# One inference step of a hybrid encoder: scale products moved within a step, element-wise work moved between engines, a new order at the start

## The chip, the cores and the metric

One core of a Trainium2 chip runs the kernel. The metric is the device time of one execution in microseconds (us), the median of several runs. Engines are named as in the profile: PE is TensorE, with PEld its weight loads, DVE is VectorE, ACT is ScalarE, POOL is GpSimd, SP is the queue that issues the DMAs.

## The reference

One layer (DEPTH = 1) is computed for two groups of tokens that share the weights: a prompt of 256 and a sample of 32 tokens, both of width 2048. In short:

```python
def trunk_layer(x, mk, mv, past_k, past_v, lru_buf, lru_h, ssd_buf, ssd_h, ffn_buf, lp):
    m, st = hybrid_mixer(rmsnorm(x, lp['norm_mix']), past_k, past_v, lru_buf, lru_h, ssd_buf, ssd_h, lp)
    h = x + m
    h = h + cross_attn(rmsnorm(h, lp['norm_xattn']), mk, mv, lp['w_xq'], lp['w_xo'])
    f, ffn_new = conv_ffn(rmsnorm(h, lp['norm_ffn']), ffn_buf, lp['w_up'], lp['ffn_conv_w'], lp['ffn_conv_b'], lp['w_down'])
    return h + f, st + (ffn_new,)

def hybrid_mixer(xn, ...):
    proj = xn @ lp['w_in']          # 2048 -> 13840: q k v, lru x/gate, ssd z/xBC/dt, 3 merge gates
    o_a = stick_breaking(q, k_all, v_all, P)                       # 8 heads x 128
    o_b = rg_lru(causal_dwconv(lx, ...)) * gelu(lg)                # width 1024, conv of 4
    o_c = rmsnorm((ssd_chunked(silu(causal_dwconv(xbc, ...))) + d * xh) * silu(z))
    merged = sum over n of sigmoid(gate_n) * (branch_n @ w_branch[n])
    return merged @ lp['w_out'], states

def conv_ffn(xn, buf, w_up, cw, cb, w_down):
    u, buf_new = causal_dwconv(xn @ w_up, buf, cw, cb)             # 2048 -> 2 x 5632, conv of 3
    g, v = jnp.split(u, 2, axis=-1)
    return (jax.nn.silu(g) * v) @ w_down, buf_new
```

`rmsnorm` scales by the root of the mean square and a gain. `causal_dwconv` is a depthwise convolution over time that also returns the last inputs as a state. The prompt's memory (256 tokens) is normed and projected to keys and values; the sample has cached ones. All is float32. The outputs are the two normed results, the keys and values, and the states.

## The kernel before

Activations lie transposed: 128 features in the partitions, 256 + 32 = 288 tokens in a row, so a width of 2048 is 16 tiles. The weights stream from memory once, 1 MB at a time. A unit of this stream is an *item*. `items` is a written list, and `run_items` (L458) walks it.

An item of the f16 form (mode "h") is 128 x 2048 float32 weights. To keep float32 accuracy from f16 products, weights and activations are each split into a high part and a low part, and three products are added: high by high, high by low, low by high. The weights are first scaled by a power of two. Its exponent is worked out in a chain over four engines: ACT squares the whole item into `junk` with a sum per partition (`square_w`, L315); PE multiplies the sums with a matrix of ones, a product with one column, into `z` (`scale_mm`, L328; for a group of four items DVE adds the sums into `sum` first); DVE masks the exponent into `e` (`scale_e`, L338); ACT and POOL make `scale` and `inv` of it (`scale_w`, L342). Then follow the high part `wh` (`split_high`, L351: on DVE for every third item, else on ACT) and the low part `wl` on DVE (`split_low`, L366). `z` has one PSUM buffer. An item is 48 products with 288 columns.

An item of the f32r form (mode "r") is 128 x 1024 weights or less. Its parts are f32r numbers, with no square, no scale and no `z`. It is used while the norm is not known yet: the products take x times its gain, and the norm's factor `S` is applied when the result is read (`ev`, L523). The first `R_IN` = 6 projections of `w_in` and the first `R_UP` = 6 of `w_up` are of this form. Each is 48 products, in two or three items.

A *step* is the time of one item on PE. `stream` (L387) gives four parts p0 to p3, which `run_items` calls after each quarter of the item's products (an f32r item of 24 products has two stretches with two parts each). After each stretch `tick` (L425) lets every side step go one `yield` further; evictions, convolutions, attention heads, the scan and the splits of activations are such steps. p0 issues the high part of the second item ahead, p1 its low part, the load of the sixth item ahead and the product into `z` for the third ahead, p2 the square of the fourth ahead and `e`, p3 `scale` and `inv`. An item in `needs` that isn't over makes `finish` (L431) tick until it is.

The order on PE, ACT, DVE and POOL is the order in which the program writes the instructions, so an instruction that waits holds all that stand behind it on its engine. All DMAs, results and caches included, are issued on SP's queue. There are 5 weight buffers of 1 MB, 6 buffers for split parts, 55 activation tiles, 4 PSUM banks for projections and 3 for side work.

`conv` (L710) reads a projection in PSUM: DVE multiplies the taps by the two scales into `wt` and writes the state (`last`), ACT makes the first tap `cx`, DVE adds the others, and the bank is freed. `split_normed` (L1196) makes of a normed activation tile `t` (DVE), the f16 high part `h` (ACT) and the low part `l` (DVE, L283); it serves the inputs of `w_in`, `w_xq` and the f16 part of `w_up`. `normed_later` (L1158) adds squares of the residual for the next norm and, ahead of the FFN, makes its f32r parts `xh` (ACT) and `xl` (DVE).

The start is written out (L1654 to L1695): loads, splits of the first weights and of the inputs, squares of the 16 input tiles on ACT, 15 adds one after the other on POOL (L560), then the norm's products, for which PE waits in place.

Of the kernel before, what the change touches and what calls it, by code (L numbers as in the profile page):

```python
# [16 lines left out]
P = 128  # L17
# [3 lines left out]
D = 2048  # L21
# [32 lines left out]
R_IN, R_UP = 6, 6  # L54
# [42 lines left out]
class Group:  # L97


    def __init__(self, n):  # L100
        self.n, self.got, self.sq, self.scale, self.inv = n, 0, None, None, None

# [18 lines left out]
def encoder_step(ctx: ExitStack, tc: tile.TileContext, A):  # L121
# [228 lines left out]

    def split_high():  # L351
        it = items[split_at[0]]
        n = it.n
        split_at[0] += 1
        if it.mode == "r":
            it.h = wh_p.tile([P, 1024], F32R, tag="wh", name=nm("wh"))
            act(it.h[:, 0:n], it.raw[:, 0:n], AF.Copy)
        elif it.mode == "h":
            it.h = wh_p.tile([P, 2048], F16, tag="wh", name=nm("wh"))
            if split_at[0] % 3 == 0:  # L360
                V.tensor_scalar(it.h[:, 0:n], it.raw[:, 0:n], it.scale, None, ALU.mult)  # L361
            else:
                act(it.h[:, 0:n], it.raw[:, 0:n], AF.Copy, scale=it.scale)
        return it
# [22 lines left out]
    def stream(i):  # L387

        high, scales = [], []

        def p0():
            while split_at[0] < ahead(i, 2):
                high.append(split_high())

        def p1():
            for it in high:
                split_low(it)
            while raw_at[0] < ahead(i, NRAW + 1):
                fetch_w()
            while sc_at[0] < ahead(i, 3):  # L400
                it = scale_mm()
                scales.append(it)

        def p2():
            while sq_at[0] < ahead(i, 4):
                square_w()
            for it in scales:
                scale_e(it)

        def p3():  # L410
            for it in scales:
                scale_w(it)
        return p0, p1, p2, p3

    side = []
# [15 lines left out]
    def finish(get):  # L431
        while get() is None or not get().over:
            tick()
# [65 lines left out]
    def add_r(srcs, xh, xl, done, n=T, needs=(), pre=None):  # L499
# [3 lines left out]
        for c, x in enumerate(srcs):  # L503
            nk = x.shape[1] // P
            items.append(Item("r", [x], [still(u, xh, xl, n, k0, nk, 0, c == 0, c == len(srcs) - 1)],
                              needs=needs if c == 0 else (), pre=pre if c == 0 else None))
# [111 lines left out]
    def sb_evac(kind, h):  # L618
        def done(u):
            x = tt(name=kind)  # L620
# [5 lines left out]
            if kind == "v":  # L626
                sb["g", h] = spawn(sb_head(h))
        return done
# [81 lines left out]
    def conv(u, n, w, b, hist, last):  # L710
# [7 lines left out]
        else:  # L718
            wt = small("wt", 4)
            V.tensor_scalar(wt[:, 0:n], w, u.inv, u.inv2, ALU.mult, ALU.mult)  # L720
            w = wt
        tail = src[:, 257 - n:321 - n].rearrange("p (a b) -> p a b", b=32)[:, :, 0:n - 1]
        if u.inv is None:
            G.tensor_copy(last, tail)
        else:
            V.tensor_scalar(last, tail, u.inv, u.inv2, ALU.mult, ALU.mult)  # L726
# [431 lines left out]
    def normed_later(j, h, key, name, op, parts=None):  # L1158

        if parts:  # L1160
            act(parts[0][:, C], h, AF.Copy, scale=pc(name, j))
# [8 lines left out]
        if parts:  # L1170
            stt(parts[1][:, C], h, pc(name, j), f32(parts[0])[:, C], ALU.mult, ALU.subtract)
# [24 lines left out]
    def split_normed(op, xs, name, scale, n=T):  # L1196
# [4 lines left out]
        for i, x in enumerate(xs):  # L1201
            y = tt()
            stt(y[:, 0:n], x, g[:, i:i + 1], scale[:, 0:n], ALU.mult, ALU.mult)
            op.h[i], op.l[i] = split16(y[:, 0:n], n)
# [203 lines left out]
    def xo_evac(j, half):  # L1408
        def done(u):
# [5 lines left out]
            hh_[j], hl_[j] = tt(F32R, "xh"), tt(F32R, "xl")  # L1415
            yield
            yield from normed_later(j, h[:, C], "f", "g_ffn", op_f, (hh_[j], hl_[j]))
# [197 lines left out]
    def up(b):  # L1615
        j0, n = blocks[b]
        for j in range(j0, j0 + n):
            for i, done in ((j, up_g(j)), (NFF + j, up_v(j))):
                if 2 * j < R_UP:
                    add_r(two("w_up", i), hh_, hl_, done)  # L1620
# [52 lines left out]
    make_sb_masks()  # L1673
    for k in range(KD):
        if k >= 8:
            split_x([k])
        add_square(acc, xin[k][:, C], k == 0)
        if k == 9:
            run_items(0, 2)
        if k == 13:  # L1680
            run_items(2, 4)
    run_items(4, 6)
    spawn(gains("g_mix", gmix))
    run_now(norm_scale(acc, S, D))
# [158 lines left out]
```

## Time and profile before

| what | value |
|---|---|
| median of 3 runs | 2322.0 us (2319.89 to 2324.35) |
| profiled execution | 2324.89 us |
| its span | 2323.2 us |
| mean granted clock of PE | 0.97 |
| busy: PE, DVE, ACT, POOL | 2192.3, 1639.1, 1571.4, 312.8 us |
| bytes moved | 409.32 MB, mean 176 GB/s |

The span runs from the first to the last instruction of one profiled execution. A busy time is the sum over an engine's instructions; products on PE overlap, and their ends are modelled. The granted clock is a share of TensorE's full level. A wait in a row is idle time of an engine just before an instruction, put down to the instruction that ended last.

### The profile page before, as it was taken

What the parts mean: (1) busy time and instruction counts of PE and PEld (TensorE: products, weight loads), DVE (VectorE), ACT (ScalarE), POOL (GpSimd) and SP (SyncE); (2) the same over time, 40 slices, a digit from 0 to 9 for tenths busy, and PEclk for the clock granted to TensorE, in tenths of its full rate; (3) what the DMA queues carried; (4) which work ended last, traced back from release to release, by engine and by line L of the source; (5) the groups of instructions that cost most, each with busy time, mean ns of one, the idle gap of its engine ahead of it and who ended that gap; (6) DMA issues with size and microseconds to landing.
All of it is one profiled execution on the core that took longest, in us unless ns stands there. A gap on an engine that the chain in (4) does not pass through costs nothing.

```text
span 2323.2 us, 43464 instructions
## 1 busy us (share of the span) xinstructions
PE 2192.3 (94%) x17375; PEld 1739.6 (75%) x17375; DVE 1639.1 (71%) x2561; ACT 1571.4 (68%) x2261; POOL 312.8 (13%) x723
## 2 busy tenths in 40 slices
PE   6899978999899999899899999969999999999997
PEld 6788756777677777676587768867777777777776
DVE  5666776668875556765656556778887878878775
ACT  5666688777777685775555556657776767767674
POOL 3000001212232241132100000300000000000002
PEclk8899989999999999999899999979999999999999
DMA  7455434766556565565455554345555555555551
GB/s 234 160 177 165 159 121 145 241 222 215 167 190 202 186 214 189 160 216 169 160 182 183 183 177 166 110 145 182 164 185 179 182 182 174 175 180 180 182 183 62
DMA packets 134124, 409.32 MB, mean 176 GB/s; under 512 B 15264, under 2 KB 36896, under 8 KB 133920
## 3 DMA queue, kind: packets, MB, share of 16 engines
q1 hardware_dynamic: 133920, 406.53, 53.8%
q8 instruction: 136, 2.23, 0.4%
q14 instruction: 68, 0.56, 0.1%
HBM read 396.26 MB, written 10.21 MB: 175 GB/s over the span
## 4 chain that ended last, share of the span: by engine, by line
PE 74%; DVE 12%; ACT 9%; issue 3%; DMA 2%; POOL 1%; SPq 0%; POOLq 0%; DVEq 0%; ACTq 0%
PE mm L191 70%; DVE wl L194 4%; PE sd L191 3%; ACT wh L169 3%; ACT junk L169 2%; DVE cx L194 2%; ACT t L169 1%; ACT h L169 1%; ACT L169 1%; DVE wh L361 1%; DVE t L194 1%; POOL acc L560 1%; DMA wr<-in_w_xv 1%; DVE wl L370 0%; DVE l L283 0%
## 5 line engine op out<-in xcount | busy, mean ns | idle before, releaser
L191 PE MATMUL mm<-h,wh 128*128 128x288 f16 (+1 forms) x5072 | 1458.4, 288 | 4.9 <-ACT h L169 4.9
L191 PE MATMUL mm<-l,wh 128*128 128x288 f16 (+1 forms) x5072 | 1458.3, 288 | 1.2 <-DVE l L283 0.4
L191 PE MATMUL mm<-h,wl 128*128 128x288 f16 (+1 forms) x5072 | 1458.4, 288 | 0.0
L191 PEld LDWEIGHTS <-wh 128*128 128x128 f16 x10144 | 977.7, 99 | 275.2 <-issue 29.2
L194 DVE SCALAR_TENSOR_TENSOR wl<-wr,scale,wh 128x2048 f16<-128x2048 f32 x333 | 787.3, 2364 | 254.0 <-ACT wh L169 235.5
L169 ACT ACTIVATE junk<-wr 128x2048 bf16<-128x2048 f32 x333 | 632.4, 1899 | 2.5
L191 PEld LDWEIGHTS <-wl 128*128 128x128 f16 x5072 | 499.5, 98 | 130.2 <-issue 3.5
L169 ACT ACTIVATE wh<-wr,scale 128x2048 f16<-128x2048 f32 x222 | 443.2, 1996 | 83.4 <-PE mm L191 78.3
L275 POOL TENSOR_SCALAR inv<-e 128x1 int32<-128x1 int32 x337 | 84.0, 249 | 1678.2 <-DVE e L248 1605.7
L169 ACT ACTIVATE scale<-e 128x1 int32<-128x1 int32 x337 | 65.7, 197 | 218.7 <-DVE e L248 217.0
L194 DVE SCALAR_TENSOR_TENSOR cx<-mm,wt,cx 128x1 f32<-128x1 f32 (+4 forms) x346 | 141.9, 410 | 50.1 <-ACT cx L169 41.4
L361 DVE TENSOR_SCALAR wh<-wr,scale 128x2048 f16<-128x2048 f32 x111 | 144.1, 1298 | 32.5 <-ACT scale L169 30.4
L191 PE MATMUL z<-sq,bones 128*128 128x1 bf16 x317 | 53.1, 167 | 77.9 <-ACT junk L169 54.1
L194 DVE SCALAR_TENSOR_TENSOR xre<-mm,uinv,xre 128x288 f32<-128x288 f32 x144 | 72.8, 512 | 62.8 <-PE mm L191 43.9
L169 ACT ACTIVATE cx<-mm,par,wt 128x288 f32<-128x288 f32 x102 | 60.3, 591 | 57.7 <-DVE fcv L726 45.2
L560 POOL TENSOR_TENSOR acc<-acc,t 128x288 f32<-128x288 f32 x57 | 75.4, 1323 | 72.6 <-ACT t L169 70.8
L191 PE MATMUL mm<-xh,wh 128*128 128x288 f32 x192 | 65.7, 342 | 13.7 <-ACT wh L169 8.7
L191 PEld LDWEIGHTS <-bones 128*128 128x128 bf16 x337 | 32.8, 98 | 55.3 <-DVE e L248 46.3
L191 PE MATMUL mm<-xh,wl 128*128 128x288 f32 x192 | 63.9, 333 | 4.3 <-DVE wl L370 4.3
L191 PEld LDWEIGHTS mm<-xh,wh 128*128 128x128 f32 x192 | 42.4, 221 | 32.9 <-issue 17.9
L169 ACT ACTIVATE h<-t 128x288 f16<-128x288 f32 x48 | 21.1, 439 | 65.9 <-DVE t L194 65.9
L169 ACT ACTIVATE gate<-mm,uinv 128x288 f32<-128x288 f32 x48 | 23.7, 494 | 61.3 <-PE mm L191 58.7
(324 smaller groups left out, 1854.8 us busy)
## 6 DMA issues: line engine op xcount, KB each, us to landing
wr<-in_w_in SPq DMA_DIRECT2D x215, 512.0 KB, 4.4
wr<-in_w_up SPq DMA_DIRECT2D x176, 512.0 KB, 4.3
wr<-in_w_dn SPq DMA_DIRECT2D x80, 512.0 KB, 4.4
wr<-in_w_xv SPq DMA_DIRECT2D x64, 512.0 KB, 5.1
wr<-in_w_br SPq DMA_DIRECT2D x48, 512.0 KB, 4.5
wr<-in_w_xk SPq DMA_DIRECT2D x32, 512.0 KB, 4.5
wr<-in_w_out SPq DMA_DIRECT2D x32, 512.0 KB, 4.4
wr<-in_w_xq SPq DMA_DIRECT2D x32, 512.0 KB, 4.2
```

Source lines behind the costliest of these rows:

```text
L169: return nc.scalar.activation(out, in_, f, **kw)
L191: PE.matmul(out, lhsT, rhs, start=start, stop=stop, skip_group_check=True)
L194: V.scalar_tensor_tensor(out, a, s, b, op0, op1)
L275: G.tensor_scalar(s, e, float(UNSCALE_BITS + (more << 23)), None, ALU.add)
L361: V.tensor_scalar(it.h[:, 0:n], it.raw[:, 0:n], it.scale, None, ALU.mult)
L560: G.tensor_tensor(accum[:, 0:n], accum[:, 0:n], q[:, 0:n], ALU.add)
```

## The change

Seven edits, in the order of the diff: the first nine projections of `w_in` are f32r instead of six; half of the high parts go to DVE, except in the FFN and in 28 items from the SSD's first on, where it stays a third; the parts of a step are in another order, with `e`, `scale` and `inv` first (of the products of the step before), then the high parts, then low parts, loads and squares, and the products into `z` last; the taps are scaled by two POOL instructions a tick earlier, and the state is written by ACT; ahead of the FFN, POOL multiplies by the gain (`hg`), ACT rounds it to the high part, DVE subtracts, and the f32r items wait (`Ready`) until 8 and 16 tiles are written; the low parts `l` of `split_normed` go to POOL (those of the memory, L1244, stay on DVE); at the start the squares follow the splits, their adds alternate between POOL and DVE in two sums, and the norm is a side step, for which `sb_evac` waits. In `add_r` the preload of an item is moved to its last part.

```diff
--- before.py
+++ after.py
@@ -51,7 +51,7 @@
 RG_ENDS = (3, 7)
 NRAW, NWH, NT, NU, NS, NSD = 5, 6, 55, 66, 13, 3
 
-R_IN, R_UP = 6, 6
+R_IN, R_UP = 9, 6
 
 
 SLOT = 12
@@ -99,6 +99,20 @@
 
     def __init__(self, n):
         self.n, self.got, self.sq, self.scale, self.inv = n, 0, None, None, None
+
+
+class Ready:
+
+
+    def __init__(self, h, l, n):
+        self.h, self.l, self.n = h, l, n
+
+    def __call__(self):
+        return self
+
+    @property
+    def over(self):
+        return None not in self.h[:self.n] and None not in self.l[:self.n]
 
 
 class Step:
@@ -348,6 +362,10 @@
         elif it.mode == "h":
             it.scale, it.inv = g.scale, g.inv
 
+    def high_on_dve(i):
+
+        return i % 3 == 0 if i > i_ffn or i_ssd < i < i_ssd + 28 else i % 2 == 0
+
     def split_high():
         it = items[split_at[0]]
         n = it.n
@@ -357,7 +375,7 @@
             act(it.h[:, 0:n], it.raw[:, 0:n], AF.Copy)
         elif it.mode == "h":
             it.h = wh_p.tile([P, 2048], F16, tag="wh", name=nm("wh"))
-            if split_at[0] % 3 == 0:
+            if high_on_dve(split_at[0]):
                 V.tensor_scalar(it.h[:, 0:n], it.raw[:, 0:n], it.scale, None, ALU.mult)
             else:
                 act(it.h[:, 0:n], it.raw[:, 0:n], AF.Copy, scale=it.scale)
@@ -386,32 +404,33 @@
 
     def stream(i):
 
-        high, scales = [], []
+        high = []
 
         def p0():
+            for it in scales:
+                scale_e(it)
+            for it in scales:
+                scale_w(it)
+            scales.clear()
+
+        def p1():
             while split_at[0] < ahead(i, 2):
                 high.append(split_high())
 
-        def p1():
+        def p2():
             for it in high:
                 split_low(it)
             while raw_at[0] < ahead(i, NRAW + 1):
                 fetch_w()
-            while sc_at[0] < ahead(i, 3):
-                it = scale_mm()
-                scales.append(it)
-
-        def p2():
             while sq_at[0] < ahead(i, 4):
                 square_w()
-            for it in scales:
-                scale_e(it)
 
         def p3():
-            for it in scales:
-                scale_w(it)
+            while sc_at[0] < ahead(i, 3):
+                scales.append(scale_mm())
         return p0, p1, p2, p3
 
+    scales = []
     side = []
 
     def spawn(gen, first=False):
@@ -429,7 +448,7 @@
                 side.remove(s)
 
     def finish(get):
-        while get() is None or not get().over:
+        while not (get() and get().over):
             tick()
 
     def run_now(gen):
@@ -503,7 +522,7 @@
         for c, x in enumerate(srcs):
             nk = x.shape[1] // P
             items.append(Item("r", [x], [still(u, xh, xl, n, k0, nk, 0, c == 0, c == len(srcs) - 1)],
-                              needs=needs if c == 0 else (), pre=pre if c == 0 else None))
+                              needs=needs[c:c + 1], pre=pre if c == len(srcs) - 1 else None))
             k0 += nk
 
     def add_unit(srcs, op, done, n=T, needs=(), pre=None, more=0, both=False):
@@ -617,6 +636,8 @@
 
     def sb_evac(kind, h):
         def done(u):
+            while "S" not in sb:
+                yield
             x = tt(name=kind)
             ev(u, x[:, 0:T])
             free_mm(u)
@@ -625,6 +646,7 @@
                 load(A["kt" if kind == "k" else "vt"][h], x[:, 0:T])
             if kind == "v":
                 sb["g", h] = spawn(sb_head(h))
+            yield
         return done
 
     def sb_cache(h):
@@ -716,14 +738,16 @@
             ev(u, src[:, C])
             free_mm(u)
         else:
-            wt = small("wt", 4)
-            V.tensor_scalar(wt[:, 0:n], w, u.inv, u.inv2, ALU.mult, ALU.mult)
+            wt, both = small("wt", 4), small("both")
+            G.tensor_tensor(both, u.inv, u.inv2, ALU.mult)
+            G.tensor_tensor(wt[:, 0:n], w, both.to_broadcast([P, n]), ALU.mult)
             w = wt
+            yield
         tail = src[:, 257 - n:321 - n].rearrange("p (a b) -> p a b", b=32)[:, :, 0:n - 1]
         if u.inv is None:
             G.tensor_copy(last, tail)
         else:
-            V.tensor_scalar(last, tail, u.inv, u.inv2, ALU.mult, ALU.mult)
+            act(last, tail, AF.Copy, scale=both)
         act(x[:, C], src[:, C], AF.Identity, scale=w[:, n - 1:n], bias=b)
         yield
         for d in range(1, n):
@@ -1155,10 +1179,11 @@
             load(xre[j][:, C], A["xt"][j])
         return pre
 
-    def normed_later(j, h, key, name, op, parts=None):
+    def normed_later(j, h, key, name, op, parts=False):
 
         if parts:
-            act(parts[0][:, C], h, AF.Copy, scale=pc(name, j))
+            hg = tt()
+            G.tensor_scalar(hg[:, C], h, pc(name, j), 1.0, ALU.mult, ALU.mult)
         last = tt() if j == KD - 1 else None
         if j == 0:
             norm["acc"] = tt(name="acc")
@@ -1168,7 +1193,11 @@
             add_square(norm["acc"], h, j == 0)
         yield
         if parts:
-            stt(parts[1][:, C], h, pc(name, j), f32(parts[0])[:, C], ALU.mult, ALU.subtract)
+            hi, lo = tt(F32R, "xh"), tt(F32R, "xl")
+            act(hi[:, C], hg[:, C], AF.Copy)
+            yield
+            V.tensor_sub(lo[:, C], hg[:, C], f32(hi)[:, C])
+            hh_[j], hl_[j] = hi, lo
         if last:
             yield
             yield from norm_scale(norm.pop("acc"), S, D, more=[last])
@@ -1201,7 +1230,10 @@
         for i, x in enumerate(xs):
             y = tt()
             stt(y[:, 0:n], x, g[:, i:i + 1], scale[:, 0:n], ALU.mult, ALU.mult)
-            op.h[i], op.l[i] = split16(y[:, 0:n], n)
+            h, l = ut("h"), ut("l")
+            act(h[:, 0:n], y[:, 0:n], AF.Copy)
+            G.tensor_tensor(l[:, 0:n], y[:, 0:n], h[:, 0:n], ALU.subtract)
+            op.h[i], op.l[i] = h, l
             yield
 
     gain = {}
@@ -1412,9 +1444,8 @@
             free_mm(u)
             if half == 0:
                 return
-            hh_[j], hl_[j] = tt(F32R, "xh"), tt(F32R, "xl")
-            yield
-            yield from normed_later(j, h[:, C], "f", "g_ffn", op_f, (hh_[j], hl_[j]))
+            yield
+            yield from normed_later(j, h[:, C], "f", "g_ffn", op_f, True)
         return done
 
 
@@ -1617,7 +1648,7 @@
         for j in range(j0, j0 + n):
             for i, done in ((j, up_g(j)), (NFF + j, up_v(j))):
                 if 2 * j < R_UP:
-                    add_r(two("w_up", i), hh_, hl_, done)
+                    add_r(two("w_up", i), hh_, hl_, done, needs=[Ready(hh_, hl_, 8 * c + 8) for c in range(2)])
                 else:
                     add_unit(two("w_up", i), op_f, done, needs=[lambda: xa.get("f")] if 2 * j == R_UP and i == j else ())
 
@@ -1671,17 +1702,27 @@
     split_x(range(6, 8))
     split_w()
     make_sb_masks()
+    run_items(0, 2)
+    split_x(range(8, 12))
+    run_items(2, 4)
+    split_x(range(12, 16))
+
+    acc2 = tt(name="acc")
     for k in range(KD):
-        if k >= 8:
-            split_x([k])
-        add_square(acc, xin[k][:, C], k == 0)
-        if k == 9:
-            run_items(0, 2)
-        if k == 13:
-            run_items(2, 4)
+        q = (acc, acc2)[k] if k < 2 else tt()
+        act(q[:, C], xin[k][:, C], AF.Square)
+        if k > 1:
+            a = (acc, acc2)[k % 2]
+            (G, V)[k % 2].tensor_tensor(a[:, C], a[:, C], q[:, C], ALU.add)
     run_items(4, 6)
     spawn(gains("g_mix", gmix))
-    run_now(norm_scale(acc, S, D))
+
+    def first_norm(a, b):
+        yield 2
+        yield from norm_scale(a, S, D, more=[b])
+        sb["S"] = True
+    spawn(first_norm(acc, acc2), True)
+    acc2 = None
     run_items(6, 8)
     xs = [t[:, C] for t in xin]
     xa["x"] = spawn(split_normed(op_x, xs, "g_mix", S))
```

## Rows read from the trace of the kernel before

**Rows 1.** Page, part 1: busy us, share, instructions of the engines.

```profile
PE 2192.3 (94%) x17375; PEld 1739.6 (75%) x17375; DVE 1639.1 (71%) x2561; ACT 1571.4 (68%) x2261; POOL 312.8 (13%) x723
```

**Rows 2.** Waits of PE, whole span: total us, times, longest.

```profile
PE z L191 <- ACT junk L169: 54.1, 16, 8.4
PE z L191 <- DVE e L248: 22.9, 16, 3.8
PE z L191 <- DVE sum L242: 8.3, 4, 4.4
PE mm L191 <- ACT wh L169: 8.7, 4, 4.7
...
PE sd L191 <- POOL acc L560: 2.2, 2, 1.7
```

**Rows 3.** Windows by stage: length, busy by engine, PEclk, DMA share, GB/s.

```profile
0.00:115.00 115.00, 87.11 (x553) 77.03 (x554) 71.78 (x112) 66.23 (x111) 20.48 (x38) 0.85 0.62 197
...
280.00:410.00 130.00, 109.80 (x808) 82.67 (x807) 89.26 (x163) 109.90 (x162) 16.07 (x39) 0.92 0.42 137
...
1080.00:1160.00 80.00, 68.01 (x423) 42.76 (x421) 52.14 (x72) 46.50 (x64) 7.85 (x22) 0.89 0.49 158
...
1480.00:1560.00 80.00, 61.38 (x407) 55.92 (x405) 55.36 (x96) 42.83 (x70) 9.51 (x17) 0.85 0.41 130
1560.00:2280.00 720.00, 718.54 (x5951) 573.19 (x5950) 584.07 (x999) 517.52 (x706) 40.22 (x169) 1.00 0.54 177
2280.00:2323.00 43.00, 29.65 (x238) 23.04 (x235) 24.50 (x44) 20.32 (x41) 14.01 (x20) 0.90 0.16 56
```

**Rows 4.** Chain of waits, 40 us and more in: start, us, what.

```profile
29.32 9.63 PE mm L191 x72
...
2210.99 5.90 PE mm L191 x48
```

**Rows 5.** Timeline of PE at 309 us: start, length, [idle before <-releaser].

```profile
309.24 0.16 PE L191 MATMUL z<-sq,bones 128*128 128x1 bf16 x1 [5.34 <-ACT junk L169]
```

**Rows 6.** Instructions by shape, whole span: count, busy, mean ns, idle before.

```profile
L194 DVE SCALAR_TENSOR_TENSOR wl<-wr,scale,wh 128x2048 f16<-128x2048 f32 x333 | 787.3, 2364 | 254.0 <-ACT wh L169 235.5 <-DMA wr<-in_w_up 4.8 <-DMA wr<-in_w_xv 4.1
...
L169 ACT ACTIVATE wh<-wr,scale 128x2048 f16<-128x2048 f32 x222 | 443.2, 1996 | 83.4 <-PE mm L191 78.3 <-issue 3.3
L361 DVE TENSOR_SCALAR wh<-wr,scale 128x2048 f16<-128x2048 f32 x111 | 144.1, 1298 | 32.5 <-ACT scale L169 30.4 <-DMA wr<-in_w_xo 1.6 <-PE z L191 0.3
...
L370 DVE TENSOR_TENSOR wl<-wr,wh 128x1024 fp32r<-128x1024 f32 x21 | 26.6, 1270 | 9.0 <-ACT wh L169 8.0 <-DMA wr<-in_w_in 0.5 <-PE mm L191 0.5
...
L720 DVE TENSOR_SCALAR wt<-par,inv,inv 128x3 f32<-128x3 f32 x82 | 23.0, 280 | 0.0
```

**Rows 7.** The start: timeline of POOL, a window, PE's wait up to 115 us.

```profile
12.27 16.24 POOL L560 TENSOR_TENSOR acc<-acc,t 128x288 f32<-128x288 f32 x15 [8.95 <-ACT t L169]
...
47.00:111.00 64.00, 48.74 (x315) 41.10 (x314) 43.14 (x65) 39.23 (x58) 2.37 (x8) 0.81 0.49 154
...
PE z L191 <- ACT junk L169: 11.7, 3, 6.1
```

**Rows 8.** FFN entry: tile xh (min/median/max ns, first to last start); DVE timeline.

```profile
L191 PE MATMUL mm<-xh,wh x96: 288/296/610, 1493.8 to 1560.1; 128*128 128x288 f32 x96
...
1513.28 0.46 DVE L283 TENSOR_TENSOR l<-t,h 128x288 f16<-128x288 f32 x1 [0.51 <-ACT h L169]
```

**Rows 9.** POOL beside DVE: timelines near 1460 us, tile xl, line 275.

```profile
1459.70 0.80 POOL L560 TENSOR_TENSOR acc<-acc,t 128x288 f32<-128x288 f32 x1 [1.18 <-ACT t L169]
...
1462.35 2.14 POOL L560 TENSOR_TENSOR acc<-acc,t 128x288 f32<-128x288 f32 x1 [1.70 <-ACT t L169]
...
1461.48 2.35 DVE L194 SCALAR_TENSOR_TENSOR wl<-wr,scale,wh 128x2048 f16<-128x2048 f32 x1 [1.71 <-ACT wh L169]
...
L194 DVE SCALAR_TENSOR_TENSOR xl<-xre,par,xh x16: 504/520/1054, 1454.4 to 1497.3; 128x288 fp32r<-128x288 f32 x16
...
L275 POOL TENSOR_SCALAR inv<-e x337: 208/209/2370, 41.3 to 2292.9; 128x1 int32<-128x1 int32 x169
```

## The prediction

> **What bounds the kernel now.** I read the page's busy lines first: TensorE is busy 2192.3 of 2323.2 us [rows 1]. So the most that removing its idle time can give is 130.9 us, and to that comes what it loses while the throttle grants it less than full speed. Second, the waits of TensorE over the whole span: the one-column products into `z` wait 54.1 us for ScalarE's squares, 22.9 us for VectorE's `e` and 8.3 us for VectorE's `sum`, 85.3 us together. No other single wait is above 8.7 us [rows 2]. Third, the stage table says where: 27.9 us of idle up to 115 us, 20.2 between 280 and 410, 12.0 between 1080 and 1160, 18.6 between 1480 and 1560, 13.4 after 2280. In the first four the mean granted clock is 0.85 to 0.92, so the lower of the two levels (1.2 against 2.4 GHz) was granted for part of them. The 720 us of the FFN show 1.5 us of idle at clock 1.00 [rows 3]. Two results follow: the FFN can win nothing, and the rest wins only where TensorE stands still or is slowed. At the full level 48 f16 products take 5.90 us (0.123 each), and 72 f32r products 9.63 us (0.134) [rows 4].
>
> **One-column products at the end of a step.** Before, the square of item i+4 goes to ScalarE three quarters into a step and its product into `z` comes half-way through the next: three quarters of a step, 4.4 us. After, the product is behind the whole step: 5/4, 7.4 us. It has 24 products x 0.123 = 2.95 us more cover. The 5.34 us stall at 309.24 [rows 5] would be 2.4 us if ScalarE's backlog is the same. `e` moves ahead of the two long VectorE instructions (2.36 us low part, 1.30 high part [rows 6]) from behind them, with the product still three quarters of a step later; waits for `e` should mostly go. `sum` stays just ahead of its product and gains a quarter step, 1.5 us. What pays: the low part is issued a quarter step later, so its reserve before use falls from 1.5 to 1.25 steps (8.9 to 7.4 us). That is what is late next: waits of `mm` for `wl`. The loads are issued a quarter step later too, on SP's one queue with the cache loads and K/V stores; the square reads them two steps on, 11.8 us, which covers it at 1 MB each.
>
> Idle outside the start, the FFN entry, the FFN and the tail is 130.9 - 27.9 - 18.6 - 1.5 - 13.4 = 69.5 us, nearly all at `z`. The bounds are a loss of 10 (if the later low part costs 1.5 us at half a dozen bursts) and a gain of 69.5 plus some 30 for the slowed stretches. Five bursts or more lose 3 us of wait each and the `e` waits go: 32 us. Slowed stretches that no longer follow: about 10. Waits that come back at the operands: -14. I take **-28**, nearest to the row of the one stall that I can work through.
>
> **Half of the high parts on VectorE.** A high part costs ScalarE 2.00 us and VectorE 1.30 [rows 6]. About 186 of the 333 items lie outside the FFN and the SSD stretch; a sixth of them, some 31, change engine: ScalarE -62 us, VectorE +40 us, over 1400 us. Between 280 and 410 the squares-only items sit on every fourth index, so two of three high parts instead of one go to VectorE: about 6 x 2.0 = 12 us off a ScalarE that is busy 109.9 of 130 [rows 3]. It is counted within the -28. In stretches where VectorE is the fuller engine it costs; bounds -10 to +5.
>
> **Conv taps and tails.** 102 convs: VectorE loses two instructions of 0.28 us each, `wt` [rows 6] and the tail beside it. GpSimd gains two small ones, ScalarE a small scaled copy, and the bank is freed a quarter step later, with four banks. 82 of these lie in the FFN, hidden by TensorE's 718.5 of 720 us [rows 3]: **0**. If the cover goes, it is because `cx` on ScalarE waits for GpSimd; behind it queue the high part and the square, and TensorE waits for those (second rival).
>
> **Start.** Up to 47 us the new order lets the split of the next weights run ahead of the squares: the 4.7 us wait for `wh` [rows 2] should go, and the GpSimd chain of 15 adds (16.24 us [rows 7], with 1.7 us of TensorE waiting at its end) is halved and no longer holds the norm's product. I take 6 us. From 47 to 111 us TensorE did 315 products in 64 us; at 0.134 that is 42, a loss of 22. The split of the normed x sits there, `t`, `h`, `l` in turn, then three projections in the f16 form whose products into `z` wait 11.7 us behind ScalarE [rows 7]. With nine projections in the f32r form these have no square, no scale and no `z`, and their 12 added items leave 24 ticks for 16 splits. VectorE needs 1.27 us per item for the low part [rows 6] and, by my estimate from the `l` of 0.46, some 1.8 for two `t`, the eviction and a share of a head, plus half a microsecond of waiting for the high part, like `l`'s [rows 8]: 3.6 us, against TensorE's 24 x 0.134 = 3.2: a little short, so I leave 8 us of loss: gain 14. Together **-20** (bounds +10 and -34). The f32r form costs 3 x 48 x (0.134 - 0.123) = **+1.6**.
>
> **FFN entry.** The f32r products run from 1493.8 to 1560.1 us [rows 8]: 66 us for 288 x 0.134 = 38.6. Per projection VectorE spends 11.5 us, among it four `l` of 0.46, each after 0.51 of waiting for `h` [rows 8]. With `l` on GpSimd these four pairs (3.9 us) go, leaving 7.6 and then some blocking by GpSimd. Four projections x 3.9 = 15.6, and the three products waiting on squares there also have more cover. GpSimd has four `l` per 8 us, at 0.8 to 2.1 each [rows 9]. The new wait for 8, then 16, finished tiles adds at most the chain `hg`, `hi`, `lo` of the last tile, some 2 to 3 us, behind one item of 3.2. **-15** (bounds +5 and -28). At the cross attention's `xq` the same edit is within the -28.
>
> Sum: -28 - 20 + 1.6 - 15 = -61. The profiled execution took 2324.9 us around its span of 2323.2, 2.9 above the median of 2322.0; 2322.0 - 61 = **2261 us**.
>
> **A rule that speaks against it.** The trace shows a GpSimd add at 0.80 us alone and 2.14 us beside a 2.35 us low part, and VectorE's next `xl` at 1.05 instead of 0.52 [rows 9]. The Trainium skill ("SBUF — State Buffer", "Who interferes with whom") states that a VectorE instruction with two SBUF inputs and a GpSimd instruction that reads SBUF exclude each other, the later one waiting for the whole of the earlier. The trace agrees. By that rule each `l` moved could hold VectorE for 0.8 us to save it 0.46; three sets of 16 would then give back about 16 us, and the sum would be -45, or 2277.
>
> **Rivals.**
> 1. *The bursts are volume, not delay.* ScalarE is busy 85% between 280 and 410; less waiting at `z` lets its backlog grow until `mm` waits for `wh` and `wl`. For it: those waits exist already at the FFN entry. Against: they total under 15 us over the span [rows 2]. Half of each gain stays: 2322 - 8 - 10 - 9 = **2295**.
> 2. *The taps on GpSimd hold ScalarE in the FFN: slower.* A small GpSimd instruction takes 0.21 us but up to 2.37 [rows 9]. Two in a row can take 4.7; a quarter step, 1.5 us, is hidden; ScalarE is free (720 - 517.5)/122 steps = 1.66 us per step [rows 3]. It decides from a mean above 3.1 us for the pair. At 4.0 each conv costs 0.86: 82 x 0.86 = 70, giving **2331**. Against: the median is 0.21. The same rule on the shared port stands behind this one.
> 3. *The start doesn't do what it says.* The inputs and their two parts already fill 48 of 55 large buffers; three more projections hold 32 of them longer, so the splits wait for buffers and, as now, SP's queue behind them. The start costs 10 instead of giving 20: **2291**.
> 4. *Everything at once.* The idle and the slowed stretches go almost entirely: **2225**.
>
> **How the numbers follow.** Forecast 0.50 (its own range 2236 to 2284), first rival 0.22, second 0.10, third 0.08, fourth 0.10. Outside 2212 to 2316 lie most of the second rival and the edges of the others, under 2 in 10. A change below 0.2% (4.6 us) can't be told from none in this kernel. Slower holds the second rival and a little of the first, 0.11; the same 0.05 from the first and third; faster 0.84.
>
> **What would show it.** Right: waits of `z` for ScalarE below 25 us and for `e` below 8; no wait of TensorE for the adds at the start, and the first f16 projection begun before 90 us having three more behind it; f32r products of the FFN entry within 52 us; 1560 to 2280 still without idle. Wrong: `mm` waiting for `wl` or `wh` by more than 25 us in all, `cx` on ScalarE waiting over 1.7 us per conv for `wt`, a longer `t` or `wl` beside GpSimd, or idle in the FFN.

## The result, and the profile after

The changed kernel takes 2290.11 us (median of 4 runs, 2288.57 to 2290.83) against 2320.94 for the kernel before in the same session: ratio 0.9864, 95% interval 0.9847 to 0.9881. The forecast was 2261 us: the direction held, the size came out at half of it. The profiled execution has a span of 2287.8 us, and TensorE is idle for 114.5 us of it, not for 130.9 [rows 1].

```profile
PE 2173.3 (95%) x17374; PEld 1730.6 (76%) x17374; DVE 1640.6 (72%) x2351; ACT 1501.7 (66%) x2322; POOL 508.1 (22%) x980
```

TensorE's waits over the span of the kernel after (total us, times, longest), to be held against [rows 2]:

```profile
PE z L205 <- DVE e L262: 24.9, 13, 4.3
PE z L205 <- ACT junk L183: 13.5, 5, 4.6
PE mm L205 <- ACT wh L183: 10.7, 4, 6.3
PE mm L205 <- POOL l L1235: 8.8, 5, 3.4
PE sd L205 <- DVE decay L1055: 7.1, 2, 6.5
PE mm L205 <- DVE wl L388: 6.6, 9, 1.6
PE z L205 <- DVE sum L256: 6.3, 3, 2.9
```

The waits of `z` fell from 85.3 to 44.7 us: a quarter is left of those for the squares, while those for `e` are about as large in total as before (24.9 against 22.9). New or larger are `wh`, GpSimd's `l`, `decay` and `wl`, 33.2 us. The same windows as [rows 3]; the kernel now reaches the later ones earlier, so their content is shifted, and the last one reaches past the end of the FFN:

```profile
0.00:115.00 115.00, 95.14 (x653) 86.83 (x654) 74.43 (x111) 67.24 (x116) 32.10 (x45) 0.94 0.65 212
...
280.00:410.00 130.00, 112.24 (x849) 85.23 (x847) 94.34 (x153) 105.37 (x155) 38.08 (x49) 0.93 0.46 152
...
1080.00:1160.00 80.00, 68.85 (x464) 46.49 (x463) 52.50 (x63) 45.65 (x68) 28.62 (x37) 0.89 0.48 161
...
1480.00:1560.00 80.00, 71.48 (x538) 62.78 (x537) 65.42 (x106) 58.03 (x93) 24.72 (x42) 0.98 0.56 179
1560.00:2280.00 720.00, 712.64 (x5909) 568.63 (x5906) 549.04 (x829) 516.68 (x787) 111.70 (x336) 1.00 0.51 169
```

A table on one scale needs a mark that both kernels pass. All kernels here issue the same products into the `mm` banks in nearly the same order, so the count of these in windows of 5 us, summed from the start, says how far a kernel has come. A product that runs over the edge of a window is counted in both, so a mark is a count of this kind and some 6% above the true number of products. Each number is the change of a stage's length against the kernel before, in us, worked out by interpolation from such windows; stages are named by the count at their end:

| kernel | start to 600 | branch 0 to 2350 | SSD to 4350 | branches to 6350 | memory to 7100 | out, xk, xv, xq, xo to 10350 | FFN entry to 11100 | FFN to 16850 | all |
|---|---|---|---|---|---|---|---|---|---|
| length before | 125.9 | 257.1 | 281.1 | 238.7 | 104.4 | 479.9 | 119.5 | 671.9 | 2278.5 |
| after | -11.5 | -5.8 | +4.0 | +0.1 | +6.7 | -9.8 | -16.6 | -2.7 | -35.6 |
| new order alone (e1) | -2.8 | -7.7 | +10.1 | -0.4 | +4.4 | -7.0 | -10.9 | +10.6 | -3.7 |
| after, old order (e2) | -4.3 | +0.5 | +7.5 | -0.2 | -2.0 | -6.7 | -4.2 | +47.2 | +37.9 |
| low parts alone (e3) | +1.3 | -0.9 | +2.3 | -1.1 | -0.6 | -6.4 | -5.3 | -0.7 | -11.5 |
| after, thirds (e4) | -12.3 | -2.3 | -1.7 | -0.7 | +4.4 | -13.2 | -17.3 | -2.4 | -45.5 |
| start alone (e5) | +1.2 | +3.8 | +1.3 | -0.5 | -0.2 | -0.3 | -0.1 | -1.2 | +4.0 |
| after, taps on DVE (e6) | -12.1 | -5.1 | +6.4 | -0.5 | +5.0 | -10.3 | -16.2 | +10.8 | -22.1 |
| after, xq's `l` on DVE (e7) | -11.5 | -5.5 | +3.8 | -0.7 | +4.8 | -6.6 | -15.8 | -2.2 | -33.7 |
| after, parameters early (e8) | -11.2 | -4.9 | +4.1 | -0.8 | +6.0 | -14.1 | -16.5 | -2.8 | -40.1 |
| e4 and e8 (e9) | -11.2 | -4.1 | -0.3 | -0.1 | +6.6 | -15.3 | -17.3 | -2.3 | -44.2 |
| e9, memory and start (e10) | -19.9 | -3.5 | -1.5 | -0.2 | -3.0 | -15.7 | -17.2 | -2.6 | -63.6 |
| old order, `e` first (e11) | -6.2 | +0.2 | +0.4 | +0.3 | -2.7 | -4.0 | -5.7 | +50.3 | +32.6 |
| and `scale` first (e12) | -0.8 | +6.5 | +20.9 | +14.1 | +9.5 | +2.8 | -0.5 | +75.0 | +127.9 |

Two cautions. Each row compares one profiled execution with one of the kernel before, which took 2324.89 us, 1 to 4 above the medians of that kernel; a row's last number lies 2 to 5 us below what the medians give (-35.6 against -30.8 for the changed kernel; for e10 10 us), and the difference of two rows is the better measure. And when each product is counted once, by its start, single cells move by up to 3.4 us; where that matters it is said.

The changed kernel won at the start, at the FFN entry and before it, and lost 10.7 us in the SSD and memory stages.

### The profile page after: what moved, and what is told of

Same layout as the page of the kernel before. It is cut to its first block, busy times and chain, and to the rows that moved or that the text cites. A ratio compares the mean times of both kernels' runs of the same rounds, so it can differ in the third digit from the quotient of the medians.

```text
span 2287.8 us, 43633 instructions
## 1 busy us (share of the span) xinstructions
PE 2173.3 (95%) x17374; PEld 1730.6 (76%) x17374; DVE 1640.6 (72%) x2351; ACT 1501.7 (66%) x2322; POOL 508.1 (22%) x980
## 4 chain that ended last, share of the span: by engine, by line
PE 74%; DVE 11%; ACT 8%; issue 4%; DMA 1%; POOL 1%; SPq 0%; POOLq 0%; DVEq 0%; ACTq 0%
PE mm L205 71%; DVE wl L208 3%; PE sd L205 3%; ACT wh L183 2%; ACT junk L183 2%; DVE cx L208 1%; DVE wh L379 1%; DVE t L208 1%; ACT L183 1%; ACT t L183 1%; ACT h L183 1%; DVE wl L388 1%; DVE l L208 0%; DVE decay L1055 0%; DMA wr<-in_w_in 0%
## 5 line engine op out<-in xcount | busy, mean ns | idle before, releaser
L205 PE MATMUL mm<-l,wh 128*128 128x288 f16 (+1 forms) x5024 | 1441.2, 287 | 10.9 <-POOL l L1235 8.8
L205 PE MATMUL mm<-h,wh 128*128 128x288 f16 (+1 forms) x5024 | 1441.0, 287 | 2.7 <-ACT h L183 2.3
L205 PE MATMUL mm<-h,wl 128*128 128x288 f16 (+1 forms) x5024 | 1441.5, 287 | 0.0
L205 PEld LDWEIGHTS <-wh 128*128 128x128 f16 x10048 | 965.4, 99 | 258.0 <-issue 16.8
L183 ACT ACTIVATE wh<-wr,scale 128x2048 f16<-128x2048 f32 x184 | 367.3, 1996 | 11.3 <-PE mm L205 4.8
L379 DVE TENSOR_SCALAR wh<-wr,scale 128x2048 f16<-128x2048 f32 x146 | 192.8, 1321 | 59.1 <-ACT scale L183 58.9
L488 POOL TENSOR_TENSOR uinv<-inv,inv 128x1 f32<-128x1 f32 x152 | 96.4, 634 | 7.1
L205 PE MATMUL mm<-xh,wh 128*128 128x288 f32 x240 | 76.3, 318 | 16.1 <-ACT wh L183 10.7
L205 PE MATMUL z<-sq,bones 128*128 128x1 bf16 x314 | 52.7, 168 | 39.4 <-DVE e L262 24.9
L262 DVE TENSOR_SCALAR e<-z 128x1 int32<-128x1 int32 x318 | 48.3, 152 | 49.3 <-PE z L205 48.1
L205 PE MATMUL mm<-xl,wh 128*128 128x288 f32 x240 | 74.0, 308 | 0.0
L1235 POOL TENSOR_TENSOR l<-t,h 128x288 f16<-128x288 f32 x48 | 56.2, 1177 | 57.3 <-ACT h L183 57.2
```

What stands on the lines that cost most here:

```text
L183: return nc.scalar.activation(out, in_, f, **kw)
L205: PE.matmul(out, lhsT, rhs, start=start, stop=stop, skip_group_check=True)
L262: V.tensor_scalar(e, ps[:, 0:1].bitcast(I32), 1, HALF_EXP, ALU.logical_shift_right, ALU.bitwise_and)
L488: G.tensor_tensor(inv, it.inv, it.op.inv, ALU.mult)
L1235: G.tensor_tensor(l[:, 0:n], y[:, 0:n], h[:, 0:n], ALU.subtract)
```

## The experiments

The delay theory is the forecast's: the waits at `z` are a matter of cover, so the new order of the step is what wins. The volume theory is its first rival: in the bursts VectorE and ScalarE have more to do than the time holds. Medians and ratios are against the kernel before in the same session; its median lay between 2320.94 and 2323.67 us, so medians of different sessions are compared to some 3 us at best.

**e1, only the new order of the step, on the kernel before** (in short; the functions are those of the diff).

```diff
 p0: -split_high          +scale_e, scale_w (of the last step's products)
 p1: -split_low, fetch_w, scale_mm   +split_high
 p2: -square_w, scale_e   +split_low, fetch_w, square_w
 p3: -scale_w             +scale_mm
```

> Only the new order of the parts of a step, on the kernel before. Delay theory (the forecast's: waits at z are a matter of cover): some 25 to 30 us faster, about 2294. Volume theory (the bursts hold more work than VectorE and ScalarE can do in the time, and TensorE waits for the next thing): 3 to 10 us faster, 2311 to 2318; the waits of z for ScalarE fall by half or more, and those for e or of mm for wl rise by nearly as much.

2322.93 us, ratio 0.9997 (0.9988 to 1.0006): no change, where both theories had a gain. The waits at `z` moved as the volume theory says, to be held against [rows 2]:

```profile
PE z L191 <- DVE e L248: 45.4, 25, 4.9
PE z L191 <- ACT junk L169: 19.5, 6, 5.0
```

Those for the squares fell by 34.6 us, those for `e` rose by 22.5. The table shows sums of both signs: the order wins 7.7, 7.0 and 10.9 us in the stages with bursts and loses 10.1 in the SSD and 10.6 in the FFN, where convolutions run. The cover was real at the FFN entry; in the middle it was spent elsewhere.

**e2, the changed kernel with the old order.** The diff is e1's, turned round, on the kernel after.

> The changed kernel with the old order of the parts of a step. Delay theory: loses 25 us or more, 2315. Volume theory: loses 3 to 10 us, 2293 to 2300, and most of it where the bursts are ScalarE's squares.

2364.45 us, ratio 1.0177 (1.0160 to 1.0194), worse than either theory had it: 74 us slower than the changed kernel, 50 of them in the FFN, a stage that I had taken for one in which nothing moves. The chain of waits there (start, us, what):

```profile
1612.45 2.01 ACT wh L183
1614.49 2.35 DVE wl L208
1616.84 0.44 DVE cx L208
1617.31 0.53 DVE cx L208
1617.86 0.23 DVE cx L208
1618.11 0.22 DVE cx L208
1618.33 0.08 DVE e L262
1618.42 0.07 ACT t L183
1618.49 0.28 issue
1618.77 0.20 ACT scale L183
1618.99 2.01 ACT wh L183
1621.03 2.35 DVE wl L208
```

There is no TensorE in it. It is a ring over two engines (a chain that leads from an instruction back to the same one of the next item): high part 2.0, low part 2.35, the convolution's adds 1.5, `e`, ScalarE's `tanh` of the adds' result, `scale`, the next high part, 6.54 us from 1612.45 to 1618.99 against 5.90 for TensorE's step. The step shown is a common one: between the FFN's first and last convolution the starts of `wl` lie 6.35 us apart in the mean, most often 6.5, against 5.85 in the changed kernel. With taps and tail a tick ahead of them, a convolution's adds come a quarter step later, which in the old order is behind the low part; before, they were ahead of it.

**e3, only the low parts, on the kernel before** (in short).

```diff
 split_normed: -op.h[i], op.l[i] = split16(y)
+              act(h, y, AF.Copy); G.tensor_tensor(l, y, h, ALU.subtract)
 normed_later: hg on G, hi on ACT, lo on DVE; Ready for 8 and 16 tiles
```

> On the kernel before only the low parts of the normed activations on GpSimd (and the FFN's f32r parts by way of hg, with the waits for 8 and 16 tiles). Volume theory: the FFN entry gives most of its 19 us here, 2300 to 2308. Delay theory: the entry's gain is largely cover at z, so 5 to 8 us here, 2313.

2314.33 us, ratio 0.9963 (0.9950 to 0.9975). At the FFN entry it wins 5.3 us, not most of the stage's gain, as the delay theory said, whose 2313 is also met; the new order alone wins 10.9 there, and the two sum to 16.2 of the changed kernel's 16.6.

**e4, a third of the high parts on VectorE everywhere.**

```diff
-        return i % 3 == 0 if i > i_ffn or i_ssd < i < i_ssd + 28 else i % 2 == 0
+        return i % 3 == 0
```

> The changed kernel with a third of the high parts on VectorE everywhere. Delay theory: ScalarE's backlog is back, 8 to 12 us slower, 2300. Volume theory: between 280 and 410 it loses some 4 us, between 890 and 1000, where VectorE is the fuller engine, it wins back about as much: 2288 to 2292.

2281.58 us, ratio 0.9822 (0.9805 to 0.9839): 8.5 us *faster* than the changed kernel, outside both expectations. More high parts on VectorE win 3.5 us in branch 0 and lose 12.2 from there to the end of the out and xk to xo stage (2.1 and 9.8 with each product counted once). In the SSD, the memory and that last stage VectorE is the fuller of the two engines.

**e5, only the start, on the kernel before**: `R_IN = 9`, the new order of squares and adds, the norm as a side step.

```diff
-R_IN, R_UP = 6, 6
+R_IN, R_UP = 9, 6
...
-    run_now(norm_scale(acc, S, D))
+    spawn(first_norm(acc, acc2), True)
```

> On the kernel before only the start: nine f32r projections, the new order of squares and adds, the norm as a side step. If the 11 us by which the changed kernel is ahead at 115 us are the start's own: 2309 to 2312. If they need the low parts on GpSimd or the new order of the step: 2314 to 2320.

2330.47 us, ratio 1.0029 (1.0018 to 1.0041): slower, and outside both expectations. The start by itself wins nothing; it needs the other edits, the order of the step above all: with all edits but the order it wins 4.3 us up to the mark 600 (e2), with the order 11.5.

**e6, taps and tails on VectorE.** The functions `conv` of before in the kernel after.

```diff
-            G.tensor_tensor(both, u.inv, u.inv2, ALU.mult)
-            G.tensor_tensor(wt[:, 0:n], w, both.to_broadcast([P, n]), ALU.mult)
+            V.tensor_scalar(wt[:, 0:n], w, u.inv, u.inv2, ALU.mult, ALU.mult)
...
-            yield
...
-            act(last, tail, AF.Copy, scale=both)
+            V.tensor_scalar(last, tail, u.inv, u.inv2, ALU.mult, ALU.mult)
```

> The changed kernel with taps and tails on VectorE as before. If the move costs nothing and gives nothing, as forecast: 2288 to 2292. If GpSimd's taps hold ScalarE in the convs of the first half: 3 to 6 us faster, 2285. If VectorE's relief in the SSD stretch counts: 3 to 6 us slower.

2305.41 us, ratio 0.9923 (0.9911 to 0.9936): 15 us slower than the changed kernel and outside all three expectations; the FFN alone loses 13.5, where it was to cost nothing. ScalarE's and TensorE's waits of this kernel between 1600 and 2250 us:

```profile
PE z L205 <- DVE e L262: 10.3, 10, 2.9
...
ACT cx L183 <- DVE fcv L748: 68.9, 71, 1.9
ACT scale L183 <- DVE e L262: 64.2, 44, 3.1
```

`cx` waits on ScalarE for VectorE's tail (`fcv`), 71 times, and `z` for `e`. With taps on GpSimd and the tail on ScalarE the first two rows are gone. In e1, which has the same order and the same `conv`, that wait of `cx` is 69.7 us, 72 times, and the FFN loses nearly the same: 10.6 there, 10.8 here, both against the kernel before.

**e7, the low parts ahead of `w_xq` on VectorE.**

```diff
-            G.tensor_tensor(l, y, h, ALU.subtract)
+            (V if name == "g_x" else G).tensor_tensor(l, y, h, ALU.subtract)
```

> The changed kernel with the low parts ahead of w_xq on VectorE again; the other two sets stay on GpSimd. TensorE waits 8.8 us for GpSimd's l there. If GpSimd is too slow beside VectorE: 4 to 8 us faster, 2283. If VectorE then takes as long (the volume theory): within 2 us.

2293.02 us, ratio 0.9869 (0.9852 to 0.9885), no difference that the intervals tell from the changed kernel: VectorE takes as long, or a little longer (the stage with `w_xq` loses 3.2 us).

**e8, the FFN's parameters one stage earlier.**

```diff
+    make_ffn_params()
     xa["m"] = spawn(merged_split())
     run_items(i_xk, i_xq)
     xa["smp"] = spawn(sample_gen())
-    make_ffn_params()
```

> The changed kernel with the FFN's parameters (4.7 us of GpSimd between the l of w_xq) made one stage earlier. If GpSimd's queue is what TensorE waits for at w_xq: 3 to 5 us faster, 2286. If VectorE's volume is: within 1 us.

2287.83 us, ratio 0.9850 (0.9836 to 0.9864). The stage that holds `w_xq` gains 4.3 us; the median moved 2.3, between the two expectations, and the intervals overlap, so the total alone does not show it.

**e9, e4 and e8 together.**

> The changed kernel with a third of the high parts on VectorE everywhere and the FFN's parameters made one stage earlier. If what the two won by themselves adds up (8.5 and 2.3 us): 2279. If both relieve the same wait at w_xq: 2282.

2281.99 us, ratio 0.9828 (0.9815 to 0.9842), no more than e4 alone: they don't add up.

**e10, e9 with the memory's low parts on GpSimd, and items 4 and 5 ahead of the squares.**

```diff
-            op_mem.h[j], op_mem.l[j] = split16(r[:, M], NP_)
+            act(h[:, M], r[:, M], AF.Copy)
+            G.tensor_tensor(l[:, M], r[:, M], h[:, M], ALU.subtract)
...
     split_x(range(12, 16))
+    run_items(4, 6)
     for k in range(KD):          # squares
...
-    run_items(4, 6)
```

> The one before, and also: the memory's 16 low parts on GpSimd, and two items of the start ahead of the squares. Volume theory: between the products 6350 and 7100 VectorE has 6.9 us less to do and TensorE gains 3 to 6; at the start the 6.35 us wait for wh goes and half of it stays won: 2271 to 2275. If the waits for e there are delay and not volume, no gain at the memory; if the start is bound by its loads, none there: 2279.

2268.32 us (2266.67 to 2269.38), ratio 0.9772 (0.9759 to 0.9785): faster than both kernels, 22 us ahead of the changed one, and 3 us ahead of what even the volume theory had. Against e9 the start gives 8.7 us, the memory stage 9.6 (6.6 and 9.2 with each product counted once). The rows for the start, ahead of 115 us, after and e10:

```profile
PE mm L205 <- ACT wh L183: 10.7, 4, 6.3
```

```profile
PE mm L205 <- ACT wh L183: 3.2, 5, 1.2
```

The one wait of 6.3 us was for high parts that stood behind 16 squares on ScalarE, and it went with the squares' place.

**e11, the old order with `e` right behind its product.**

```diff
                 it = scale_mm()
                 scales.append(it)
+                scale_e(it)
```

> The changed kernel with the old order of the parts of a step (2364 us), but e right behind its product into z, ahead of the next convolution's adds on VectorE. If the 47 us that the old order lost in the FFN come from e standing behind low part and adds: the FFN is without idle again or nearly, 2315 to 2330. If GpSimd's taps and inv are what is late there: 2355 to 2365.

2357.27 us, ratio 1.0154 (1.0140 to 1.0168): the FFN still loses 50. The place of `e` alone was not it. The time lies where GpSimd's taps and `inv` were to put it, but the traces speak against them: in the FFN no wait of ScalarE, VectorE or TensorE is put down to GpSimd here, and in e2 one, of `cx` for `wt`, 0.2 us. I turned to the ring that e2's chain shows.

**e12, e11 with `scale` ahead of ScalarE's square.**

```diff
         def p2():
+            for it in scales:
+                scale_w(it)
             while sq_at[0] < ahead(i, 4):
                 square_w()

         def p3():
-            for it in scales:
-                scale_w(it)
+            scales.clear()
```

> The old order with e behind its product (2357 us), and scale ahead of ScalarE's instruction that waits for the convolution's adds. Ring theory: in the FFN a ring over two engines runs 6.6 us a step (high part 2.0, low part 2.35, adds 1.5, the square or tanh of their result on ScalarE, scale, next high part); with scale ahead of that square the ring is 4.7 and hidden by the 5.9 us of TensorE, so the 50 us lost in the FFN fall below 10: 2310 to 2320. If the ring is not it (GpSimd's inv and taps, or VectorE's volume): 2350 to 2358.

2454.24 us, ratio 1.0555 (1.0540 to 1.0569), far on the other side of both expectations. My ring of 4.7 us left out what stands between `scale` and the next high part on ScalarE. The chain of e12:

```profile
1712.60 2.34 DVE wl L208
1714.94 0.08 DVE e L262
...
1715.04 0.04 ACT scale L183
...
1715.15 2.00 ACT junk L183 x2
...
1717.71 0.85 ACT h L183 x2
1718.56 1.90 ACT wh L183
...
1720.48 2.35 DVE wl L208
```

Low part, `e`, `scale`, then the square of a whole item with the reading of its sum (2.0), a small square left out above (0.56 with its wait), 0.85 of `h`, the high part, the next low part: 7.88 us from 1712.60 to 1720.48. This step is one of the longest; the mean between the FFN's convolutions is 6.60 us. The edit put the square inside the ring. So in both kernels the chain that sets the step shown runs over these two engines and not over TensorE, and my account of which instructions belong to it was wrong the first time. No run took one of them out and brought the old order back to 5.9 us, so that the ring costs the 50 us is read from the chains and not shown by an edit.

## Why the prediction came out at half

**The sum by its terms.** Forecast -28 in the middle, -18.4 at the start with the f32r form's cost, -15 at the FFN entry, 0 in the FFN. By the table: -4.8 from product 600 to 10350, -11.5, -16.6, -2.7. Nearly all that is missing by the table, 23 of some 26 us, is the middle. Of its -28, 10 stood for stretches that the clock no longer slows: the granted clock went from 0.92 to 0.93 between 280 and 410 us and stayed at 0.89 between 1080 and 1160. It rose at the start (0.85 to 0.94) and at the FFN entry (0.85 to 0.98), where no term names it [rows 3].

**The step that failed** is "Five bursts or more lose 3 us of wait each and the `e` waits go: 32 us", less 14 for "Waits that come back at the operands". Five times 3 us and all 22.9 for `e` would be 37.9; which share of the `e` waits the 32 takes is not said. In the middle the order alone gives 0.6 us (e1: -3.4 at 10350 less -2.8 at 600), and 3.9 beside the other edits (after against e2). Most of the squares' waits did go, but waits for `e` did not: VectorE came to `e` late, wherever `e` stood in the step. Around the memory's splits TensorE stops at one item after another, before and after (timelines of PE; start, length, what, idle before and its releaser):

```profile
921.18 0.16 PE L191 MATMUL z<-sq,bones 128*128 128x1 bf16 x1 [3.48 <-ACT junk L169]
...
931.99 0.16 PE L191 MATMUL z<-sq,bones 128*128 128x1 bf16 x1 [3.08 <-ACT junk L169]
...
942.67 0.16 PE L191 MATMUL z<-sq,bones 128*128 128x1 bf16 x1 [2.98 <-ACT junk L169]
```

```profile
910.64 0.18 PE L205 MATMUL z<-sq,bones 128*128 128x1 bf16 x1 [4.20 <-DVE e L262]
...
921.67 0.19 PE L205 MATMUL z<-sq,bones 128*128 128x1 bf16 x1 [3.28 <-DVE e L262]
...
931.95 0.18 PE L205 MATMUL z<-sq,bones 128*128 128x1 bf16 x1 [2.86 <-DVE e L262]
```

One wait took the other's place at about the same length: the first rival's mechanism. Taking 16 small subtractions off VectorE gave 9.6 us there (e10), where the order gave nothing. That shows that VectorE's queue is what was late. It does not show that VectorE had more work than time: from 905 to 965 us after, it is busy for 45.4 of 60 us (the third number) and stands in place, waiting for ScalarE, for most of the rest:

```profile
905.00:965.00 60.00, 47.83 (x369) 36.67 (x368) 45.43 (x72) 33.03 (x67) 12.00 (x23) 0.91 0.40 129
```

```profile
DVE l L297 <- ACT h L183: 6.1, 11, 0.9
DVE wl L208 <- ACT wh L183: 5.2, 2, 2.6
```

Over the whole stage the 16 subtractions hold VectorE for 7.5 us of work and 9.1 of waiting for `h`, and `e` stands behind both. What e10 won has two parts: TensorE's idle time in the stage falls by 5.7 us against e9, its busy time by 3.9, while the mean granted clock is 0.97 instead of 0.94. How much of it is due to the work taken away and how much to the waits was not run apart.

Of the signs named for being right, `z` for ScalarE below 25 us (13.5), f32r products of the FFN entry within 52 and the FFN without idle came; `z` for `e` below 8 us did not (24.9), nor a first f16 product before 90 us (93.7). That the forecast's direction held and its size by half is in part luck: the 10.7 us lost in the SSD and memory stages, part of the high parts' 8.7 among them, were met by gains elsewhere that were in part priced for another reason. So it is with the first rival's 2295, 5 us off: its terms were -8, -10 and -9 where -4.8, -11.5 and -16.6 were measured.

**The high parts** were counted within the middle, bounded at -10 to +5. They cost 8.7 us net (e4 against after, between the marks 600 and 10350), outside that bound. The reason stood in the prediction, "In stretches where VectorE is the fuller engine it costs", without a size.

**The taps** were put at 0, "hidden by TensorE's 718.5 of 720 us". Taps and tails put back into the changed kernel cost 15 us (e6), because the FFN's cover held only for the old order. In the FFN, against the kernel before: the new order without them loses 10.6 (e1) or 10.8 (e6), they without the new order lose 47.2 (e2), both together win 2.7. Two edits, each a loss there, are none together. The taps were never run alone on the kernel before; e2 stands for that, as the high parts keep their third in the FFN and e3 and e5 change this stage by 1.2 us or less. The second rival, GpSimd holding ScalarE, did not occur: the pair is short after (0.39 us by the medians), and no wait of `cx` for `wt` is among ScalarE's.

```profile
L743 POOL TENSOR_TENSOR wt<-par,both x102: 194/195/421, 202.2 to 2196.4; 128x3 f32<-128x3 f32 x82, 128x4 f32<-128x4 f32 x20
...
L742 POOL TENSOR_TENSOR both<-inv,inv x102: 188/192/2295, 202.0 to 2195.1; 128x1 f32<-128x1 f32 x102
```

**The start** gave 11.5 of 18.4. Its order moved the wait: the `wh` that was to go (4.7 us) came back at 6.3, behind the squares, and e10 won 8.7 us at the start by their place. From 47 to 111 us TensorE did 440 products against 315 [rows 7]:

```profile
47.00:111.00 64.00, 59.62 (x440) 54.66 (x439) 43.19 (x57) 38.50 (x60) 21.98 (x23) 0.97 0.64 205
```

**The FFN entry** was right in size and wrong in cause. The f32r products took 49.7 us against 66.3 [rows 8], within the 52 that I had named:

```profile
L205 PE MATMUL mm<-xh,wh x96: 288/295/510, 1475.4 to 1525.1; 128*128 128x288 f32 x96
```

Two thirds of the gain is the order's (e1: 10.9), a third the low parts' (e3: 5.3). The products waiting for squares there, which I mentioned in half a sentence, were the larger part: in this stage they wait 8.8 us before, 3.5 in e1, 7.6 in e3, 3.2 after. And of the stage's 16.6 us some 10 are idle time, while 6.6 are TensorE's busy time, 101.0 before and 94.4 after for the same products, at a granted clock of 0.89 and 0.98.

**The shared port.** At `w_xq`, `t` on VectorE took 0.63 us in the median beside GpSimd's `l`, not 0.51, and at most 0.99:

```profile
L208 DVE SCALAR_TENSOR_TENSOR t<-xre,sg_x,S x16: 501/626/989, 1085.6 to 1111.9; 128x288 f32<-128x288 f32 x16
```

The rule of the Trainium skill that the prediction weighed ("SBUF — State Buffer", "Who interferes with whom") agrees with these times. By it the sum would have been 2277, nearer to 2290 than mine, but not for its reason alone: the move of all low parts is a gain (e3, 9 us), and back on VectorE those of `w_xq` are no faster (e7).

## What to carry to other kernels

Before a wait is counted as won by more cover, add up what the engine behind it has to do in that stretch, and what it waits for in place: if the two together fill the time, the wait comes back under another name, as here between 905 and 965 us, and taking instructions off that engine paid where a new order did not. Where two in-order engines feed each other, follow the ring from an instruction back to itself one item later; when the ring is longer than the step of the busiest engine, it sets the step, and an edit that moves instructions across others can cost 50 us in a stage without any idle time (e2). So the parts of such a change are to be tried singly and also each taken out: here the order alone gave 0, and taken out it cost 74.

## What the runs showed of the hardware

A small subtraction on GpSimd (128x288, f16 out) takes 0.73 us alone and 2.56 to 2.71 beside a 2.35 us low part of VectorE, and VectorE's two-input instructions grow longer in turn: the 16 `t` at `w_xq` take 11.7 us together instead of 8.3, and one low part there 2.70 us. So 16 of them in a burst free less of VectorE than the 0.46 us each that they took there before. GpSimd's queue then matters as much as its speed: TensorE waited 3.42 us for an `l` behind 4.6 us of parameters. Timeline of POOL and PE after:

```profile
1086.72 0.73 POOL L1235 TENSOR_TENSOR l<-t,h 128x288 f16<-128x288 f32 x1 [14.09 <-ACT h L183]
1088.95 2.57 POOL L1235 TENSOR_TENSOR l<-t,h 128x288 f16<-128x288 f32 x1 [1.50 <-ACT h L183]
...
1108.12 1.47 POOL L1462 TENSOR_SCALAR par<-par 128x44 f32<-128x44 f32 x4
...
1112.30 0.44 POOL L730 TENSOR_TENSOR hist_f<-t,par 128x88 f32<-128x88 f32 x1
1112.70 5.82 POOL L1235 TENSOR_TENSOR l<-t,h 128x288 f16<-128x288 f32 x4
...
1113.47 0.40 PE L205 MATMUL mm<-l,wh 128*128 128x288 f16 x1 [3.42 <-POOL l L1235]
```
